# Gated linear attention: decayed q and k halves in one tile per level on VectorE, the rank-16 gate in one product, filling products in smaller pieces

## The chip, the cores and the metric

The kernel runs on one core of a Trainium2 chip. The metric is the device time of one execution in microseconds. TensorE (PE) does the matrix products, VectorE (DVE), ScalarE (ACT) and GpSimd (POOL) work on tiles of 128 partitions, SyncE (SP) starts the loads. [...]

## What is computed

Two transformer-like blocks over 512 tokens of width 1024, in fp32. The change lies in the first mixer of the second block, a gated linear attention (GLA) with 4 heads, keys of 128 and values of 256 per head:

```python
def gla_mixer(h, w_in, w_gate, b_gate, g_out, w_out):
    proj = h @ w_in                               # q, k, v, r and a rank-16 part glr
    log_a = log_sigmoid(glr @ w_gate + b_gate) / 16
    o = gla_chunked(q * DK**-0.5, k, v, log_a)
    o = rmsnorm(o, g_out) * silu(r)
    return o @ w_out

# in gla_chunked, for each chunk of 64 tokens, b = cumsum(log_a) in the chunk:
attn[i, j] = sum_c q[i, c] * k[j, c] * exp(b[i, c] - b[j, c])     # j <= i
o = (q * exp(b)) @ state + attn @ v
state = state * exp(b_last) + (k * exp(b_last - b)).T @ v
```

Before it in the same kernel stand a convolution mixer, a mixture of 16384 small experts and a gated projection; behind it an MLP, a latent attention and a second MLP.

## The kernel before

Activations lie transposed, 128 channels on the partitions and the 512 tokens along the free dimension. A product in full precision is three passes (`mm3`, L229 to L233): each operand is split into a high part in the fast fp32r format and the rest (`h`, `lo`), and high x high, low x high and high x low are added in PSUM. Weights come as blocks of 16 units of 128 x 128 through `Stream` (L75); `load_split` (L208) copies a block in two chunks to the high part on ACT (L214) and subtracts on POOL (L215) for the rest. Two blocks' splits fit in memory. PSUM has four accumulators `mm` (`ps`), two `sm` (`psm`) and two `gg`.

`gla_mix` (L1023) takes the normalized input `hs` in two halves of the tokens. `early` does projections 0 to 3 (q and k of heads 0 and 1) and beside them `low` (L1079), the rank-16 projection of 16 columns, also in three passes. Then come projection 4, the gate products of the four heads (L1095, plain fp32 on 16 rows), the log-sigmoid as Abs, Exp, Ln on ACT (L1099 to L1104), its running sum `b` within a chunk as a scan on DVE (L1107), and projections 5 and 6.

The scores with decay are built in `gla_decay` (L1149) without an exponential of a positive number: for each of six levels `s` = 32, 16, 8, 4, 2, 1 the tokens are cut into pairs of neighbouring runs of `s`; a query in the second run and a key in the first meet at the reference, the last token of the first run. `parts` (L1160) computes the distance `d` of `b` to that reference for both halves (two DVE subtractions, L1169 and L1170), takes the exponential (L1171), and multiplies q by it on DVE (`ql`, L1173) and k on POOL (`kl`, L1174), both over all 512 tokens. Four products of 128 x 128 (L1187) give a group of scores in PSUM, and a copy under a mask (L1192; the first level multiplies by its mask, L1190) takes from it what belongs to the level. The seventh step uses q and k themselves and the mask of the diagonal. The parts of the next level are computed ahead of the scores of this one. At the end come the decayed k and q for the state (L1194 to L1202) and a transpose. `gla_chain` (L1210) multiplies scores and state with v; `gate` (L1118) normalizes and multiplies with silu of r.

`weave` (L128) writes the order by hand: it steps through generators and after every n-th step calls a filling function, a v block `v_(n, half)` (48 products for four token tiles, whose sums `vp` occupy all four `mm` accumulators until the second half is done) or an r projection `r_(n)` (24 products). This order is a priority, not the order of execution: a planner fixes each engine's order at compile time, from its own estimate of when operands are ready, and may take later work first.

## Time and profile before

| | us |
|---|---|
| median of 3 runs | 3233.8 |
| lowest and highest | 3232.93, 3239.72 |
| the profiled execution | 3239.99 |
| its span, first to last instruction | 3238.2 |
| TensorE matmul busy | 3064.1 (95%) |
| mean granted clock | 0.973 |

The profile is one execution. A timeline row gives the start and the duration in us, the engine, the line of the kernel, the operation, output <- inputs, how many, and in brackets how long the engine was idle before and who released it. A group row gives busy time and mean ns of one, then the idle time before the group. Matmuls overlap, so the distance between two starts tells their cost, not their duration. The linear attention up to its output projection takes about 1978 to 2224 us.

### The profile page before, as it was taken

The numbers are of one execution on the slowest core, as the hardware profiler recorded it, in microseconds if no ns is written. First come the engines' busy times: TensorE is split into PE (matmuls) and PEld (weight loads), VectorE is DVE, ScalarE is ACT, GpSimd is POOL, SyncE is SP. The second block draws the span as 40 slices with busy tenths as digits, with TensorE's granted clock in tenths as the row PEclk, the third lists the DMA queues.
The fourth block names the chain that finished last, engine by engine and source line by source line (L and its number), as shares of the span: only waits on it lengthen the run. The fifth ranks groups of instructions, "written<-read, shape, count | busy, mean of one in ns | idle before, by whom it ended". The sixth has DMA issues, their size and how long they took to land.

```text
span 3238.2 us, 38828 instructions
## 1 busy us (share of the span) xinstructions
PE 3064.1 (95%) x15428; PEld 2552.4 (79%) x15428; DVE 1910.5 (59%) x3262; ACT 1056.2 (33%) x1632; POOL 1446.8 (45%) x777
## 2 busy tenths in 40 slices
PE   8599998889999999999999988899999999999998
PEld 7488887677888888887777777678888887888887
DVE  8974778986545555556888556765311267552123
ACT  4232223444332222322222245343322234442222
POOL 5635666222444444444444443533445431244444
PEclk9799999999999999999999998899999999999999
DMA  3122333655544544446776321111222221122321
GB/s 134 71 79 105 117 117 124 234 208 221 185 172 169 182 169 171 167 157 241 255 267 222 107 78 60 65 40 66 91 85 104 98 78 48 53 79 84 117 87 64
DMA packets 131062, 418.59 MB, mean 129 GB/s; under 512 B 7728, under 2 KB 73776, under 8 KB 97088
## 3 DMA queue, kind: packets, MB, share of 16 engines
q1 hardware_dynamic: 130880, 416.11, 36.4%
q8 instruction: 121, 1.98, 0.2%
q14 instruction: 61, 0.50, 0.0%
HBM read 364.70 MB, written 51.38 MB: 128 GB/s over the span
## 4 chain that ended last, share of the span: by engine, by line
PE 67%; DVE 13%; DMA 2%; issue 2%; ACT 1%; POOL 1%; DVEq 0%; POOLq 0%; ACTq 0%
PE mm L231 21%; PE mm L233 20%; PE mm L232 20%; DVE a L627 2%; DMA a<-act_d 2%; DVE al L630 2%; PE gg L845 2%; DVE og L827 1%; DVE o L822 1%; DVE x L641 1%; DVE l L378 1%; PE sm L1223 1%; DVE aw L926 1%; PE sm L1187 1%; DVE sq L295 0%
## 5 line engine op out<-in xcount | busy, mean ns | idle before, releaser
L215 POOL TENSOR_TENSOR wl<-raw,wh 128x1024 fp32r<-128x1024 f32 (+4 forms) x526 | 1261.5, 2421 | 1608.1 <-ACT wh L214 1596.4
L231 PE MATMUL mm<-h,wh 128*128 128x512 f32 (+1 forms) x2524 | 963.5, 382 | 27.0 <-DVE x L964 7.5
L233 PE MATMUL mm<-h,wl 128*128 128x512 f32 (+1 forms) x2524 | 956.6, 380 | 23.6 <-POOL wl L215 23.5
L232 PE MATMUL mm<-l,wh 128*128 128x512 f32 (+1 forms) x2428 | 927.7, 382 | 16.5 <-DVE l L226 12.1
L214 ACT CAST wh<-raw 128x1024 fp32r<-128x1024 f32 (+4 forms) x526 | 509.9, 996 | 1038.8 <-PE mm L232 543.6
L231 PEld LDWEIGHTS mm<-h,wh 128*128 128x128 f32 x2524 | 484.4, 192 | 114.6 <-DVE x L964 8.7
L233 PEld LDWEIGHTS mm<-h,wl 128*128 128x128 f32 x2524 | 483.6, 192 | 113.1 <-POOL wl L215 27.5
L232 PEld LDWEIGHTS mm<-l,wh 128*128 128x128 f32 x2428 | 465.5, 192 | 101.0 <-DVE l L226 12.9
L231 PE MATMUL mm<-ah,wh 128*128 128x512 f32 x1024 | 401.2, 392 | 12.8 <-DVE x L641 12.7
L233 PE MATMUL mm<-ah,wl 128*128 128x512 f32 x1024 | 400.6, 391 | 0.0
L232 PE MATMUL mm<-al,wh 128*128 128x512 f32 x1024 | 400.2, 391 | 0.0
L627 DVE TENSOR_TENSOR a<-a,g 128x512 f32<-128x512 f32 x128 | 189.0, 1498 | 261.7 <-ACT a L612 194.1
L231 PEld LDWEIGHTS mm<-ah,wh 128*128 128x128 f32 x1024 | 193.5, 189 | 56.9 <-issue 14.5
L641 DVE TENSOR_TENSOR x<-x,mm 128x512 f32<-128x512 f32 x256 | 171.0, 679 | 100.4 <-PE mm L233 100.2
L233 PEld LDWEIGHTS mm<-ah,wl 128*128 128x128 f32 x1024 | 193.1, 189 | 40.5
L232 PEld LDWEIGHTS mm<-al,wh 128*128 128x128 f32 x1024 | 193.4, 189 | 40.1
L1472 DVE TENSOR_TENSOR sg<-sg,mm 128x512 f32<-128x512 f32 (+1 forms) x48 | 30.9, 643 | 301.0 <-PE mm L233 288.0
L630 DVE TENSOR_TENSOR al<-a,ah 128x512 fp32r<-128x512 f32 x128 | 176.4, 1394 | 36.5 <-ACT ah L629 34.8
L964 DVE SCALAR_TENSOR_TENSOR x<-mm,mod,x 128x256 f32<-128x256 f32 (+1 forms) x112 | 66.5, 594 | 188.5 <-PE mm L233 188.4
L926 DVE CUSTOM_DVE_ANT_0 aw<-aw,c 128x1024 f32<-128x1024 f32 x96 | 149.5, 1557 | 11.0 <-DMA aw<-in_ada_w 11.0
L629 ACT CAST ah<-a 128x512 fp32r<-128x512 f32 x128 | 79.4, 621 | 220.7 <-PE mm L233 125.4
L231 PE MATMUL mm<-g,wh 128*128 128x512 f32 (+1 forms) x416 | 148.6, 357 | 0.0
(391 smaller groups left out, 3770.0 us busy)
## 6 DMA issues: line engine op xcount, KB each, us to landing
raw<-in_expert_u SPq DMA_DIRECT2D x64, 1024.0 KB, 4.9
raw<-in_expert_v SPq DMA_DIRECT2D x64, 1024.0 KB, 6.9
aw<-in_ada_w SPq DMA_DIRECT2D x96, 512.0 KB, 5.8
raw<-in_ffn_w_in SPq DMA_DIRECT2D x44, 1024.0 KB, 4.8
g_d<-gs SPq DMA_DIRECT2D x16, 2048.0 KB, 7.2
g<-g_d SPq DMA_DIRECT2D x32, 1024.0 KB, 6.4
act_d<-a SPq DMA_DIRECT2D x15, 1024.0 KB, 3.9
a<-act_d SPq DMA_DIRECT2D x15, 1024.0 KB, 4.8
```

The lines of the kernel that those rows point to most:

```text
L214: self.keep(nc.scalar.copy(h[:, c], raw[:, c]))
L215: nc.gpsimd.tensor_tensor(lo[:, c], raw[:, c], h[:, c].bitcast(F32), ALU.subtract)
L231: nc.tensor.matmul(out, w[0], x[0], start=start, stop=False)
L232: nc.tensor.matmul(out, w[0], x[1], start=False, stop=False)
L233: nc.tensor.matmul(out, w[1], x[0], start=False, stop=stop)
L627: nc.vector.tensor_tensor(v3(a), v3(a), g4[:, :, j, :], ALU.mult)
L629: nc.scalar.copy(h, a)
L630: nc.vector.tensor_tensor(lo, a, h.bitcast(F32), ALU.subtract)
L641: nc.vector.tensor_tensor(X[n], X[n], p, ALU.add)
L845: nc.tensor.matmul(p[:, i * P : (i + 1) * P], o1[:, t, :], og[j][:, t, :], start=(j == 0), stop=(j == 1))
L926: nc.vector.tensor_tensor_reduce(w, w, c, 1.0, 0.0, ALU.mult, ALU.add, self.mod[:, i : i + 1])
L964: self.nc.vector.scalar_tensor_tensor(x, p, self.mod[:, o + n : o + n + 1], x, ALU.mult, ALU.add)
```

## The change

Five things. `gla_decay` keeps one tile `d` per level: one DVE subtraction gives b minus the reference for both halves; the exponential is taken per half with its sign; then the first half is multiplied with k and the second with q, in place and on DVE. The scores of a level multiply the tile with itself, and the masked copy reads and writes the second halves alone. The diagonal comes first instead of last. The gate is one fp32r product on 80 rows: `w_lr` holds the 16 columns three times (at 0, 32 and 64, zeros between), so the projection gives three copies of `glr`, of which two are the high part and the third the rest, against the gate weights' high part, rest and high part. `v_` and `r_` become lists of smaller pieces (12 products each) and are handed to `weave` in another distribution, with `v_(1, 1)` behind `r_(0)` and `r_(1)`. Projection 7 is written ahead of the decay.

```diff
@@ -1027,12 +1028,15 @@
         hs = pre.hs
         masks = gl.tile([P, len(LEVELS) + 1, P], F32, tag="masks", name="masks")
         nc.sync.dma_start(masks, self.A["masks"][:, : len(LEVELS) + 1, :])
-        wg, rm = self.e("v", 8), self.e("v", 8)
-        nc.sync.dma_start(wg[:16], self.A["gla_w_gate"])
-        wl, wlh, wll = self.e("o", 4), self.e("o", 4, F32R), self.e("o", 4, F32R)
-        nc.sync.dma_start(wl[:, :P], self.A["gla_w_lr"])
-        nc.scalar.copy(wlh[:, :P], wl[:, :P])
-        nc.vector.tensor_tensor(wll[:, :P], wl[:, :P], wlh[:, :P].bitcast(F32), ALU.subtract)
+        wg, wgs, rm = self.e("v", 8), self.e("v", 8, F32R), self.e("v", 8)
+        nc.sync.dma_start(wg[:RG], self.A["gla_w_gate"])
+        nc.scalar.copy(wgs[:RG], wg[:RG])
+        lo = slice(32, 48)
+        nc.vector.tensor_tensor(wgs[lo], wg[lo], wgs[lo].bitcast(F32), ALU.subtract)
+        wl, wlh, wll = (gl.tile([P, KD, RG], dt, tag=t, name=t) for t, dt in (("lr", F32), ("lrh", F32R), ("lrl", F32R)))
+        nc.sync.dma_start(wl, self.A["gla_w_lr"])
+        nc.scalar.copy(wlh, wl)
+        nc.vector.tensor_tensor(wll, wl, wlh.bitcast(F32), ALU.subtract)
         nc.vector.memset(rm, 1.0)
         nc.vector.memset(rm.rearrange("p (c t) -> p c t", t=GCH)[:, :, 0:1], 0.0)
         sq, sv, sr = Stream(self, "gla_w_qk"), Stream(self, "gla_w_v"), Stream(self, "gla_w_r")
@@ -1049,50 +1053,56 @@
         def qk_(n):
             return lambda: evict(n, self.proj(sq, n * KD, hs))

-        vp = []
+        vp = [None] * NT

         def v_(n, half):
-            def f():
+            def f(t):
                 if half == 0:
-                    vp[:] = [self.ps() for _ in range(NT)]
-                for t, p in enumerate(vp):
-                    sl = slice(t * P, (t + 1) * P)
-                    for kk in range(half * KD // 2, (half + 1) * KD // 2):
-                        w = sv.unit(n * 32 + 4 * kk, 4)
-                        self.mm3(p, (hs[kk][0][:, sl], hs[kk][1][:, sl]), w, kk == 0, kk == KD - 1)
-                    if half:
-                        vt[t][n] = self.e("v", 8)
-                        nc.scalar.copy(vt[t][n], p)
-
-            return f
+                    vp[t] = self.ps()
+                sl = slice(t * P, (t + 1) * P)
+                for kk in range(half * KD // 2, (half + 1) * KD // 2):
+                    w = sv.unit(n * 32 + 4 * kk, 4)
+                    self.mm3(vp[t], (hs[kk][0][:, sl], hs[kk][1][:, sl]), w, kk == 0, kk == KD - 1)
+                if half:
+                    vt[t][n] = self.e("v", 8)
+                    nc.scalar.copy(vt[t][n], vp[t])
+
+            return [lambda t=t: f(t) for t in range(NT)]
+
+        rp = []

         def r_(n):
-            def f():
-                p = self.proj(sr, n * KD, hs)
-                rs[n] = self.e("r", 4)
-                nc.scalar.activation(rs[n], p, AF.Silu)
-
-            return f
+            def f(half):
+                if half == 0:
+                    rp.append(self.ps())
+                for k in range(half * KD // 2, (half + 1) * KD // 2):
+                    self.mm3(rp[-1], sr.unit(n * KD + k), hs[k], k == 0, k == KD - 1)
+                if half:
+                    rs[n] = self.e("r", 4)
+                    nc.scalar.activation(rs[n], rp[-1], AF.Silu)
+
+            return [lambda half=half: f(half) for half in range(2)]

         zp = []

         def low(k, sl):
             if k == 0:
-                zp.append(self.psm()[:16, :HS])
-            c = slice(k * 16, k * 16 + 16)
-            self.mm3(zp[-1], (wlh[:, c], wll[:, c]), (hs[k][0][:, sl], hs[k][1][:, sl]), k == 0, k == KD - 1)
+                zp.append(self.psm()[:RG, :HS])
+            self.mm3(zp[-1], (wlh[:, k, :], wll[:, k, :]), (hs[k][0][:, sl], hs[k][1][:, sl]), k == 0, k == KD - 1)

         self.early(sq, pre, evict, low)
-        glr = self.e("v", 8)
+        glr = self.e("v", 8, F32R)
+        lo = slice(64, RG)
         for z, sl in zip(zp, HALVES):
-            nc.scalar.copy(glr[:16, sl], z)
+            nc.scalar.copy(glr[:RG, sl], z)
+            nc.vector.tensor_tensor(glr[lo, sl], z[lo], glr[lo, sl].bitcast(F32), ALU.subtract)
         qk_(4)()
         for f in pre.later:
             f()
         lm = []
         for h in range(GH):
             z = self.psm()
-            nc.tensor.matmul(z, wg[:16, h * P : (h + 1) * P], glr[:16], start=True, stop=True)
+            nc.tensor.matmul(z, wgs[:RG, h * P : (h + 1) * P], glr[:RG], start=True, stop=True)
             bg = self.col("gla_b_gate", h)
             b.append(self.e(f"h{h}", 4))
             lm.append(self.e("v", 8))
@@ -1107,6 +1117,7 @@
             nc.vector.tensor_tensor_scan(a, rm, m, 0.0, ALU.mult, ALU.add)
         qk_(5)()
         qk_(6)()
+        qk_(7)()
         at, el = [None] * GH, [None] * GH

         def decay(h):
@@ -1132,12 +1143,12 @@
             yield
             yield from chain(nxt)

-        weave([decay(0)], [qk_(7), v_(0, 0)], 2)
-        weave([decay(1)], [v_(0, 1), v_(1, 0)], 3)
-        weave([decay(2), chain(0)], [v_(1, 1), r_(0), r_(1)], 2)
-        weave([decay(3), after(0, 1)], [r_(2), r_(3)], 3)
-        weave([gate(1), chain(2)], [r_(4), r_(5)], 2)
-        weave([gate(2), chain(3)], [r_(6), r_(7)], 2)
+        weave([decay(0)], v_(0, 0), 2)
+        weave([decay(1)], v_(0, 1), 2)
+        weave([decay(2), chain(0)], v_(1, 0) + r_(0))
+        weave([decay(3), after(0, 1)], r_(1) + v_(1, 1) + r_(2))
+        weave([gate(1), chain(2)], r_(3) + r_(4))
+        weave([gate(2), chain(3)], r_(5) + r_(6) + r_(7))
         late = []

         def rest():
@@ -1151,45 +1162,50 @@

         nc = self.nc
         c4 = lambda a, s: a.rearrange("p (n two s) -> p n two s", two=2, s=s)
-        v3 = lambda a: a.rearrange("p (t i) -> p t i", t=NT)
         at = at_[h] = self.e(f"h{h}", 4)
         nch = S // GCH
         b3 = bh.rearrange("p (c t) -> p c t", t=GCH)
         last = b3[:, :, GCH - 1 : GCH]

-        def parts(li):
-            if li == len(LEVELS):
-                return qh, kh
-            s = LEVELS[li]
+        def level(s):
+
+
             n = S // (2 * s)
             b4 = c4(bh, s)
-            ref = b4[:, :, 0, s - 1 : s].to_broadcast([P, n, s])
             d = self.g(name="d")
             d4 = c4(d, s)
-            nc.vector.tensor_tensor(d4[:, :, 1, :], b4[:, :, 1, :], ref, ALU.subtract)
-            nc.vector.tensor_tensor(d4[:, :, 0, :], ref, b4[:, :, 0, :], ALU.subtract)
-            nc.scalar.activation(d, d, AF.Exp, scale=1.0 / 16)
-            ql, kl = self.e("ql", 3), self.g(name="kl")
-            nc.vector.tensor_tensor(ql, qh, d, ALU.mult)
-            nc.gpsimd.tensor_tensor(kl, kh, d, ALU.mult)
-            return ql, kl
-
-        nxt = parts(0)
-        yield
-        for li in range(len(LEVELS) + 1):
-            ql, kl = nxt
-            if li < len(LEVELS):
-                nxt = parts(li + 1)
-                yield
+            ref = b4[:, :, 0, None, s - 1 : s].to_broadcast([P, n, 2, s])
+            nc.vector.tensor_tensor(d4, b4, ref, ALU.subtract)
+            for i in range(2):
+                nc.scalar.activation(d4[:, :, i, :], d4[:, :, i, :], AF.Exp, scale=(2 * i - 1) / 16)
+            for i, x in enumerate((kh, qh)):
+                nc.vector.tensor_tensor(d4[:, :, i, :], d4[:, :, i, :], c4(x, s)[:, :, i, :], ALU.mult)
+            return d
+
+        def scores(k, q):
             p = self.psm()
             for t in range(NT):
                 sl = slice(t * P, (t + 1) * P)
-                nc.tensor.matmul(p[:, sl], kl[:, sl], ql[:, sl], start=True, stop=True)
-            mk = masks[:, li, None, :].to_broadcast([P, NT, P])
-            if li == 0:
-                nc.vector.tensor_tensor(v3(at), v3(p), mk, ALU.mult)
-            else:
-                nc.vector.copy_predicated(v3(at), mk.bitcast(U32), v3(p))
+                nc.tensor.matmul(p[:, sl], k[:, sl], q[:, sl], start=True, stop=True)
+            return p
+
+        nxt = level(LEVELS[0])
+        p = scores(kh, qh)
+        eye = masks[:, len(LEVELS), None, :].to_broadcast([P, NT, P])
+        nc.vector.tensor_tensor(
+            at.rearrange("p (t i) -> p t i", t=NT), p.rearrange("p (t i) -> p t i", t=NT), eye, ALU.mult
+        )
+        yield
+        for li, s in enumerate(LEVELS):
+            d = nxt
+            if li + 1 < len(LEVELS):
+                nxt = level(LEVELS[li + 1])
+                yield
+            p = scores(d, d)
+            four = lambda a: a.rearrange("p (t n two s) -> p t n two s", t=NT, two=2, s=s)[:, :, :, 1, :]
+            mk = masks[:, li, :].rearrange("p (n two s) -> p n two s", two=2, s=s)[:, None, :, 1, :]
+            mk = mk.to_broadcast([P, NT, P // (2 * s), s])
+            nc.vector.copy_predicated(four(at), mk.bitcast(U32), four(p))
         d = self.g(name="d")
         nc.vector.tensor_tensor(
             d.rearrange("p (c t) -> p c t", t=GCH), last.to_broadcast([P, nch, GCH]), b3, ALU.subtract
@@ -1628,8 +1644,13 @@
         [w[:, o + h * P : o + (h + 1) * P] for h in range(GH) for o in (0, 512)], 1)))
     A["gla_w_v"] = _blocks(_units_moving(w[:, 1024:2048]))
     A["gla_w_r"] = _blocks(_units(w[:, 2048:3072]))
-    A["gla_w_lr"] = w[:, 3072:].reshape(KD, P, 16).transpose(1, 0, 2)
-    A["gla_w_gate"] = I["gla_w_gate_2"][0]
+    thrice = np.zeros((KD, P, RG), np.float32)
+    gate = np.zeros((RG, 512), np.float32)
+    for o in (0, 32, 64):
+        thrice[:, :, o : o + 16] = w[:, 3072:].reshape(KD, P, 16)
+        gate[o : o + 16] = I["gla_w_gate_2"][0]
+    A["gla_w_lr"] = thrice.transpose(1, 0, 2)
+    A["gla_w_gate"] = gate
     A["gla_w_out"] = _blocks(_units_parts(I["gla_w_out_2"][0]))
     A["positions"] = I["positions_2"]
     w = I["mla_w_in_2"][0]
```

## Rows read from the trace of the kernel before

**Rows 1.** Page: busy time, share of the span and instructions of the engines.

```profile
PE 3064.1 (95%) x15428; PEld 2552.4 (79%) x15428; DVE 1910.5 (59%) x3262; ACT 1056.2 (33%) x1632; POOL 1446.8 (45%) x777
```

**Rows 2.** Stretches: length, busy PE, PEld, DVE, ACT, POOL, clock, DMA share, GB/s.

```profile
2026.40:2060.60 34.20, 25.35 (x126) 20.61 (x125) 27.42 (x33) 11.61 (x18) 21.04 (x11) 0.90 0.26 92
...
2083.90:2112.30 28.40, 24.55 (x105) 18.38 (x103) 12.64 (x16) 6.98 (x11) 9.11 (x5) 0.82 0.11 38
...
2112.30:2143.40 31.10, 28.69 (x172) 24.05 (x173) 25.17 (x40) 16.32 (x23) 16.68 (x9) 1.00 0.18 65
...
2143.40:2176.00 32.60, 32.60 (x179) 25.04 (x180) 21.74 (x43) 17.28 (x24) 10.68 (x6) 0.95 0.01 4
```

**Rows 3.** Timeline of PE: neighbouring 512-column products at both clock levels.

```profile
2010.27 0.39 PE L232 MATMUL mm<-l,wh 128*128 128x512 f32 x1
...
2010.50 0.40 PE L233 MATMUL mm<-h,wl 128*128 128x512 f32 x1
...
2100.52 0.63 PE L231 MATMUL mm<-wh,h 128*128 128x512 f32 x1
...
2100.95 0.63 PE L232 MATMUL mm<-wl,h 128*128 128x512 f32 x1
```

**Rows 4.** Timeline of PE: where it waited.

```profile
2030.50 1.31 PE L1187 MATMUL sm<-ql,kl 128*128 128x128 f32 x8 [4.05 <-POOL kl L1174]
...
2090.29 0.66 PE L1207 MATMUL sm<-ident,d 128*128 128x128 f32 x4 [2.48 <-DVE h L1192]
...
2143.34 0.62 PE L335 MATMUL sm<-ident,ry 128*128 128x128 f32 x4 [2.35 <-DVE ry L327]
```

**Rows 5.** Timeline of DVE, 2026 to 2127.

```profile
2026.08 0.41 DVE L1169 TENSOR_TENSOR d<-h 128x256 f32<-128x256 f32 x1
...
2029.24 1.48 DVE L1169 TENSOR_TENSOR d<-h 128x256 f32<-128x256 f32 x1
...
2039.56 2.42 DVE L1169 TENSOR_TENSOR d<-h 128x256 f32<-128x256 f32 x1
...
2050.71 0.73 DVE L1192 COPY_PREDICATED h<-masks,sm 128x512 f32<-128x512 uint32 x1
...
2083.18 0.69 DVE L1202 TENSOR_TENSOR h<-h,h 128x512 f32<-128x512 f32 x1
...
2126.73 0.69 DVE L1194 TENSOR_TENSOR d<-h 128x512 f32<-128x512 f32 x1
```

**Rows 6.** Timeline of POOL, 2028 to 2056.

```profile
2028.68 1.77 POOL L1174 TENSOR_TENSOR kl<-h,d 128x512 f32<-128x512 f32 x1 [3.07 <-ACT d L1171]
...
2039.31 2.39 POOL L215 TENSOR_TENSOR wl<-raw,wh 128x1024 fp32r<-128x1024 f32 x1 [2.54 <-ACT wh L214]
...
2050.20 5.59 POOL L215 TENSOR_TENSOR wl<-raw,wh 128x1024 fp32r<-128x1024 f32 x2
```

**Rows 7.** Groups from 2000 to 2225: busy us, mean ns, idle before.

```profile
L1174 POOL TENSOR_TENSOR kl<-h,d 128x512 f32<-128x512 f32 x24 | 36.3, 1511 | 59.5 <-ACT d L1171 33.0 <-PE sm L1187 22.7 <-PE mm L233 3.9
...
L215 POOL TENSOR_TENSOR wl<-raw,wh 128x1024 fp32r<-128x1024 f32 x22 | 56.0, 2555 | 70.9 <-ACT wh L214 63.7 <-PE sm L1187 7.2
...
L289 ACT ACTIVATE sq<-o 128x256 f32<-128x256 f32 x16 | 5.5, 418 | 0.0
```

**Rows 8.** Timeline of PE: the fourth gate product.

```profile
2011.28 1.12 PE L1095 MATMUL sm<-v,v 16*128 16x512 f32 x2
```

**Rows 9.** Timeline of ACT: the fourth Abs, a weight copy.

```profile
2013.20 0.67 ACT L1099 ACTIVATE h<-sm,cols 128x512 f32<-128x512 f32 x1
...
2018.71 1.03 ACT L214 CAST wh<-raw 128x1024 fp32r<-128x1024 f32 x1
```

**Rows 10.** Groups of PE from 2007 to 2030.

```profile
L231 PE MATMUL mm<-h,wh 128*128 128x512 f32 x24 | 9.5, 395 | 0.0
```

**Rows 11.** The chain that ended last: start, us, what.

```profile
2132.34 1.80 PE sm L1187 x16
```

More of the change, by code (lines that the diff above doesn't have):

```diff
@@ L47 @@
 GCH = 64
+RG = 80
 LEVELS = (32, 16, 8, 4, 2, 1)
```

## Prediction

> **What bounds the kernel now.** TensorE is busy 95% of the span [rows 1], so a gain can only be a stretch in which it waits, works at the lower clock, or does work that falls away. I first looked for such stretches in and around the linear attention (about 1978 to 2224 us) with the table of stretches, which gives busy time and granted clock side by side [rows 2]. From 2026.4 to 2060.6 PE is busy 25.35 of 34.20 us at clock 0.90; from 2083.9 to 2112.3 it is 24.55 of 28.40 at 0.82; from 2112.3 to 2143.4 it is 28.69 of 31.10 at full clock; from 2143.4 to 2176 it is always busy, at 0.95. [...] Two neighbouring 512-column products start 0.23 us apart at the upper level and 0.43 us apart at the lower [rows 3], so a microsecond of work at the lower level throws away half. Each lower stretch follows waits of PE, whose releasers the timeline names: 4.05 us for a `kl` of POOL, 2.48 us for a masked copy of DVE, 2.35 us for the last step of a reciprocal root on DVE [rows 4].
>
> So these stretches are set by the decay, not by PE. Its rhythm is in DVE's timeline [rows 5]: the first subtraction of a level starts at 2026.08, the next level's at 2029.24, a round of 3.2 us. Inside it DVE waits 0.69 us for the exponential, and the next subtraction, which takes 0.41 us alone, takes 1.48 us. POOL's timeline shows why [rows 6]: `kl` runs from 2028.68 to 2030.45, and the subtraction ends just after. DVE is held while POOL works. The same shows at 2039.56 (2.42 us for a 0.41 us subtraction) under the weight split that POOL began at 2039.31. The masked copy at 2050.71, whose second tensor lies in PSUM, takes its usual 0.73 us though POOL is in a split from 2050.20 on. POOL spends 36.3 us on `kl` and 56.0 us on splits here [rows 7].
>
> **Part by part.**
>
> *POOL's product goes to DVE, in halves.* Per level the old round has two subtractions of 256, one exponential of 512, one DVE product of 512 and the POOL product (24 in all, 1.51 us mean [rows 7]). The new one has a subtraction of 512 (0.69 us, as the broadcast subtraction at 2126.73 [rows 5]), two exponentials of 256 (0.42 us each, as the squares of that size [rows 7]) and two products of 256 (0.41 us each, as a subtraction of that size; back to back they start 0.34 us apart). If the second exponential runs under the first product, a round is 0.69 + 0.42 + 0.41 + 0.34 = 1.9 us with the handovers; if both products wait for both exponentials, which write interleaved halves of one tile, it is 2.2 us. The masked copy reads half as many columns: 0.73 less the 0.28 us between a 512 and a 256 operation is 0.45 us. It fits into the wait for the exponential or adds itself, so a round lies between 1.9 and 2.7 us; I take 2.2, since a copy mostly finds that wait. Six rounds are 13.2 us; with the diagonal and the three products at the end (four of 0.69 us) a head takes DVE 16 us. The splits stay, four to six in the first two heads; each can hold DVE for nothing or for all of its 2.5 us. I take half: 6 us. Two heads are 38 us. Now they take from 2026.08 to 2083.87 [rows 5], 58 us.
>
> The smallest level reads every second column of PSUM, which no row here shows; I price it like a dense copy of 256. [...]
>
> *The gate in one product.* The old gate products are fp32 and show as two records each, 1.12 us a pair [rows 8]; the new ones take a 512-column pass, 0.23 us [rows 3]. Four of them save 3.5 us of PE. The two extra subtractions on 16 partitions (256 columns, 0.41 us) stand behind the eviction of `zp` and in front of the gate; projection 4 (24 products of 0.23 us, 5.5 us of PE) hides them; without that cover they cost 0.8 us. The fourth Abs runs at 2013.20 because PE came to the fourth gate product late [rows 9]; with short products it can run about 4 us earlier. I let the decay begin at 2022 instead of 2026.
>
> *The wider rank-16 weights.* `w_lr` grows from 128 to 640 columns: its DVE subtraction to about 0.83 us (0.69 for 512 columns [rows 5] and 128 more), its ACT copy alike, and `w_gate` adds a copy on ACT and a subtraction of 512 columns on DVE. Together at most 1.5 us on each of them near 1978, where the second half of the normalization also passes. It costs nothing if it falls in DVE's holes, 2.5 us if the chain stands behind all of it and behind a load that I allow 1 us more, which no row shows; I take 1. The products themselves have 80 columns instead of 16 in the stationary operand and the same 256 moving; I cost that at nothing.
>
> *`qk_(7)` ahead of the decay.* Worth nothing: the planner already runs it there. Between 2007 and 2030 PE does 24 products of each of the three kinds [rows 10], which is projections 5, 6 and 7.
>
> *Smaller filling pieces.* No PE work changes. A v block was 48 products, 11 us at 0.23, between two levels; now a score product waits behind 12, 2.7 us. But the first two heads have two v blocks instead of three. Their PE work is 2 x 11 + 2 x 7 score groups of 0.9 us (16 records in 1.80 us [rows 11]) + 1.3 for transposes, about 36 us. PE is through its projections at 2026.4 - 3.5 = 2023 and could end them at 2059; DVE ends them at 2022 + 38 = 2060. The two meet.
>
> *Sum.* Up to the end of head 1: 2083.9 - 2060 = 24 us earlier, with one v block (11 us) not yet done and three score groups and a transpose (3.3 us) done in addition: 16 us. That would close every gap there, and PE and DVE would have to interleave perfectly; I take 10. With a head at 26 us (2.7 us rounds, every split held in full) it is 2. Behind head 1: idle 3.85 and 2.41 us and half of 10.2 + 3.3 us at the lower clock, 13 us in all [rows 2]; the wait for the reciprocal root is untouched and the clock may fall again, so I take 7, with bounds of 0 and 13. Less 1 (0 to 2.5) for the set-up: 16 us, bounds 0 and 29. The profiled execution took 3239.99 us, so 3224.0; it was 6.2 us above the median of the runs, on which the forecast stands: 3217.8.
>
> **The rivals.**
>
> *The filling is held up by PSUM* (0.29). `r_(0)` now stands between `v_(1, 0)` and `v_(1, 1)`. All four `mm` accumulators then hold open v sums until `v_(1, 1)`, so `r_(0)` and `r_(1)` can't start, `gate(0)` waits for them, and the second weight slot is taken by a block that can't be used. The next v block is split only after `v_(1, 0)`: a copy of 1.03 us [rows 9] and a POOL split of 2.56 us [rows 7] stand open. Against it: the planner moves work that is ready, as it did with `qk_(7)`, and `chain(0)` can fill. Price: the 7 us behind head 1 and 3.6 us: 3228.4, within 3224 to 3232.
>
> *DVE stays as slow as it is* (0.13), which is slower than before. All three DVE operations of the new round have two tensors in SBUF and are open to being held by a split, and the first two heads have one v block less under them. If their 58 us stay, head 1 ends at 2080 with 11 us of v left over and 3.3 us done: 3.7 us lost; with the set-up's 2.5 and one more fall of the clock (3.4 us at half) about 8 us are lost: 3242. It decides from about 54 us for two heads. Against it: in the old round each `kl` alone holds DVE for 1.1 us, and these 24 holds go. [...]
>
> *Everything closes* (0.11): 16 + 13 and no set-up cost: 3205, within 3204 to 3212.
>
> **How the numbers follow.** Forecast, 3212 to 3224: 0.47. Within 0.2% (6.5 us, about what a measurement of this kernel can tell from no change) lies what ends between 3227.3 and 3240.3. Of the PSUM rival 0.10 is faster than that and 0.19 within it. Faster 0.47 + 0.11 + 0.10 = 0.68, same 0.19, slower 0.13. The range 3206 to 3236 leaves out the slower rival and the edge of the best one.
>
> **What would show it.** Right: rounds of about 2.2 us between the new 512-wide subtractions; no POOL product in the stretch; four gate products of one record; PE idle below 8 us between 2026 and the first output product, and at most one fall of the clock. The PSUM rival shows as Silu evictions of `r_(0)` only after the last v eviction; the slower one as subtractions and products of 1.5 us and more under the splits. Wrong at the root: if the part before 1960 or behind the output projection moves, since nothing of the change lies there.

## The result and the profile after

The changed kernel takes 3206.73 us (median of 5 runs, 3202.11 to 3215.19) where the kernel before takes 3233.8 (5 runs, 3232.71 to 3244.94): the two medians divide to 0.9916, and the ratio on record with its interval is 0.9928, 0.9909 to 0.9947. The forecast was 3217.8, the range 3206 to 3236. The direction came out as forecast and the mechanism in the main; the gain is larger than its 16 us, and the median lies only 0.7 us inside the range.

The profiled execution after took 3206.3 us (span 3204.5), the one before 3239.99 (span 3238.2). I split this difference at two marks that lie outside every edit: the first product of the spread (`sm<-ident,ry`, which brings the reciprocal root to all partitions) of the normalization's first half ahead of the attention, and the first of the spread of its second half ahead of the MLP. What lies between is called **the stage** from here on. Before, it runs from 1955.15 to 2275.34, which is 320.19 us. PE's timeline of the kernel after:

```profile
1943.58 1.00 PE L336 MATMUL sm<-ident,ry 128*128 128x128 f32 x4 [4.61 <-DVE ry L328]
...
2243.02 0.40 PE L336 MATMUL sm<-ident,ry 128*128 128x128 f32 x2
```

That is 299.44 us, so 20.75 us of the 33.7 us between the spans were gained in the stage. Of the rest, 11.6 us lie ahead of it and 1.4 us behind it. Ahead of it the instructions of every engine stand in the same order in both kernels, and later runs put the start anywhere from 1939 to 1960 us whatever was edited (the same kernel once more: 1946.16). So I take the 11.6 us for a difference between executions and compare stages; that is argued, not shown, and what makes the executions differ there stays open.

Where PE stood in the stage, from its records (gaps between them; half of the time in which it worked at the lower clock; the remainder as work at full clock): before 27.0 + 13.3 + 279.9 us, after 17.5 + 9.8 + 272.1. Half, because the granted clock, a share of its upper level, reads 0.50 in the falls (after: 2022.3 to 2025.6 and 2233.9 to 2240.6; before: 2096 to 2102) and 1.00 between the two of after (2025.8 to 2233.7). Each of the three fell: waits by 9.5, clock by 3.5, work by 7.8.

The stretches of the kernel after (length; busy PE, PEld, DVE, ACT, POOL; granted clock; DMA share; GB/s), which answer to [rows 2]: the first two heads of the decay, the third, the fourth, and from there into the output projection.

```profile
2015.70:2049.20 33.50, 30.17 (x171) 26.05 (x170) 29.99 (x57) 17.75 (x40) 9.88 (x4) 0.95 0.22 81
2049.20:2086.00 36.80, 34.25 (x206) 27.82 (x205) 21.38 (x38) 13.49 (x28) 9.87 (x4) 1.00 0.13 45
2086.00:2114.10 28.10, 28.10 (x150) 22.62 (x148) 19.98 (x47) 16.07 (x26) 5.22 (x2) 1.00 0.08 28
2114.10:2196.90 82.80, 80.87 (x433) 65.24 (x433) 38.53 (x78) 26.30 (x43) 21.88 (x9) 1.00 0.17 61
```

PE is idle 3.3, 2.6, 0 and 1.9 us in them, and only the first has a lower clock (0.95 of 33.5 us is 3.4 us at the lower level). The stretch at 0.82 and the one at 0.95 of [rows 2] are gone.

DVE's timeline after, which answers to [rows 5]:

```profile
2015.71 1.26 DVE L1178 TENSOR_TENSOR d<-h 128x512 f32<-128x512 f32 x2
2016.89 1.42 DVE L1182 TENSOR_TENSOR d<-d,h 128x256 f32<-128x256 f32 x4
2018.24 1.28 DVE L1178 TENSOR_TENSOR d<-h 128x512 f32<-128x512 f32 x2
...
2021.56 0.45 DVE L1208 COPY_PREDICATED h<-masks,sm 128x256 f32<-128x256 uint32 x1
2021.91 2.31 DVE L1178 TENSOR_TENSOR d<-h 128x512 f32<-128x512 f32 x1
2024.14 0.44 DVE L1208 COPY_PREDICATED h<-masks,sm 128x256 f32<-128x256 uint32 x1
2024.47 2.54 DVE L1178 TENSOR_TENSOR d<-h 128x512 f32<-128x512 f32 x1
...
2032.46 0.73 DVE L1208 COPY_PREDICATED h<-masks,sm 128x256 f32<-128x256 uint32 x1 [0.37 <-PE sm L1189]
...
2041.54 2.30 DVE L1178 TENSOR_TENSOR d<-h 128x512 f32<-128x512 f32 x1
...
2048.51 0.68 DVE L1218 TENSOR_TENSOR h<-h,h 128x512 f32<-128x512 f32 x1
```

Two levels go through DVE together: two subtractions, then their four products, and the next pair of subtractions starts 2.53 us after the first (2015.71, 2018.24), without a wait for an exponential. Two heads last from 2015.71 to 2049.19: 33.5 us, against 57.8 before. What still holds DVE are the weight splits: POOL's timeline has

```profile
2007.49 5.50 POOL L216 TENSOR_TENSOR wl<-raw,wh 128x1024 fp32r<-128x1024 f32 x2 [11.39 <-ACT wh L215]
2021.30 5.16 POOL L216 TENSOR_TENSOR wl<-raw,wh 128x1024 fp32r<-128x1024 f32 x2 [8.31 <-ACT wh L215]
```

Under the second line the two subtractions take 2.31 and 2.54 us instead of 0.68, while the masked copy between them, which reads PSUM, takes its 0.44.

### The profile page after: what moved, and what is told of

It reads as the page before. It is cut to its first block, busy times and chain, and to the rows that moved or that the text cites. A ratio compares the mean times of both kernels' runs of the same rounds, so it can differ in the third digit from the quotient of the medians.

```text
span 3204.5 us, 38766 instructions
## 1 busy us (share of the span) xinstructions
PE 3047.0 (95%) x15424; PEld 2549.7 (80%) x15424; DVE 1869.2 (58%) x3265; ACT 1051.2 (33%) x1651; POOL 1420.9 (44%) x753
## 4 chain that ended last, share of the span: by engine, by line
PE 73%; DVE 8%; ACT 1%; issue 1%; DMA 0%; POOL 0%; DVEq 0%; POOLq 0%; ACTq 0%
PE mm L232 23%; PE mm L234 23%; PE mm L233 23%; PE gg L846 2%; DVE og L828 1%; DVE o L823 1%; PE sm L1189 1%; DVE l L379 1%; DVE sq L296 0%; DVE m L370 0%; PE sm L1239 0%; DMA a<-act_d 0%; PE sm L306 0%; PE gg L1266 0%; PE gg L1260 0%
## 5 line engine op out<-in xcount | busy, mean ns | idle before, releaser
L628 DVE TENSOR_TENSOR a<-a,g 128x512 f32<-128x512 f32 x128 | 155.4, 1236 | 247.8 <-ACT a L613 194.5
L631 DVE TENSOR_TENSOR al<-a,ah 128x512 fp32r<-128x512 f32 x128 | 165.4, 1308 | 36.4 <-ACT ah L630 34.7
L927 DVE CUSTOM_DVE_ANT_0 aw<-aw,c 128x1024 f32<-128x1024 f32 x96 | 171.4, 1786 | 10.1 <-DMA aw<-in_ada_w 10.1
L232 PE MATMUL mm<-g,wh 128*128 128x512 f32 (+1 forms) x416 | 148.6, 357 | 0.0
L233 PE MATMUL mm<-g,wh 128*128 128x512 f32 (+1 forms) x416 | 148.2, 356 | 0.0
```

Source lines behind the costliest of these rows:

```text
L232: nc.tensor.matmul(out, w[0], x[0], start=start, stop=False)
L233: nc.tensor.matmul(out, w[0], x[1], start=False, stop=False)
L628: nc.vector.tensor_tensor(v3(a), v3(a), g4[:, :, j, :], ALU.mult)
L631: nc.vector.tensor_tensor(lo, a, h.bitcast(F32), ALU.subtract)
L927: nc.vector.tensor_tensor_reduce(w, w, c, 1.0, 0.0, ALU.mult, ALU.add, self.mod[:, i : i + 1])
```

## The experiments

All of them are compared by the stage (one trace each) and by the ratio to the kernel before with its interval. The two agree: the difference of stages, divided by 3240 us, lies within the interval of the ratio, or at its edge (a_only, k_half_on_pool), for every kernel below. The fourth column is the time from the first subtraction of the decay to the end of the last product of its second head; the fifth is what DVE waited for score products ahead of its 24 masked copies, from the groups of DVE.

The stage has parts that no edit of the decay or of the filling touches, and they aren't equally long in all traces: from its start to the spread of the second half 27.7 to 30.2 us, its last part, from the first half's spread ahead of the MLP, 18.0 to 19.5 us, by where the clock falls. Between the two, ahead of the decay, the clock is at its lower level for 13.7 us in kl_on_dve and 10.2 in c_only, elsewhere for at most 3.4. The third column, **decay to MLP**, runs from the first subtraction of the decay to the first half's spread ahead of the MLP and leaves these parts out. There is one trace of each kernel (two of after), so no difference of 2 or 3 us in either column is shown to be the edit's.

| kernel | ratio [95%] | stage, us | decay to MLP, us | two heads, us | DVE waits for scores, us |
|---|---|---|---|---|---|
| before | 1 | 320.19 | 231.19 | 57.8 | 9.4 |
| after | 0.9928 [0.9909, 0.9947] | 299.44 | 207.85 | 33.5 | 18.2 |
| after_again | 0.9932 [0.9909, 0.9955] | 299.49 | 207.88 | | |
| a_only: new decay | 0.9970 [0.9955, 0.9985] | 315.44 | 223.71 | 49.1 | 40.4 |
| c_only: new filling | 1.0033 [1.0017, 1.0048] | 330.86 | 239.51 | 53.6 | 15.9 |
| a_c: decay and filling | 0.9942 [0.9924, 0.9959] | 299.76 | 209.96 | 34.1 | 17.8 |
| a_b: decay and gate | 0.9975 [0.9957, 0.9994] | 311.64 | 221.43 | 46.9 | 39.1 |
| blocks_new_place | 0.9964 [0.9946, 0.9981] | 309.37 | 219.15 | 43.6 | 29.6 |
| pieces_old_place | 0.9915 [0.9885, 0.9945] | 295.33 | 205.20 | 42.1 | 22.0 |
| r_behind_v | 0.9922 [0.9899, 0.9946] | 299.75 | 209.57 | | |
| kl_on_dve | 0.9989 [0.9971, 1.0008] | 320.21 | 228.05 | 55.2 | 5.2 |
| kl_on_dve_c | 1.0020 [1.0004, 1.0036] | 327.08 | 237.32 | 60.7 | 18.4 |
| k_half_on_pool | 0.9922 [0.9896, 0.9948] | 303.44 | 212.41 | | |
| v_split_on_dve | 0.9912 [0.9883, 0.9942] | 291.81 | 205.79 | 33.7 | 14.5 |

**Which part earns it.** First the kernel after once more, for what an execution does by itself; then before with the new `gla_decay` alone (a_only) and with the new filling alone (c_only: pieces, their places, `qk_(7)`); then after with the old gate (a_c) and with the old filling (a_b). The gate alone wasn't run.

> The changed kernel once more, unchanged. If the 11.8 us by which the profiled execution of after was ahead at the start of the stage (1937.14 against 1948.92 at the same product) are a property of the program, this execution starts the stage within 3 us of 1943.6 again; if they are chance of the execution, it may start 5 to 15 us off. The stage itself: 298 to 302.

Measured: 299.49 us of stage, 0.05 from the first trace, from a start 2.6 us later. By the bound set for it, 3 us, that start speaks for a property of the program. But all kernels here run the same work ahead of the stage, and with the old gate they start anywhere from 1939.4 to 1960.1 us, with the new one from 1939.1 to 1950.6, so two executions don't settle it.

```
-  old body of gla_decay          (a_only: this alone)
+  new body of gla_decay
```

> The kernel before with the new gla_decay alone (one tile per level, all on DVE, diagonal first, half-width masked copies); gate, projection 7 and the filling as before. The stage meant here and below runs from the spread of the normalization's first half ahead of the attention (1955.15 in the trace before, 1943.58 after) to that of the second half ahead of the MLP (2275.34 and 2243.02): 320.2 us before, 299.4 after. Theory, the decay's rhythm of DVE and POOL is what was lost: stage 305 to 310, so two thirds or more of the 20.8 us come back without the rest. Rival, the filling in large blocks is what starved PE: stage 313 to 319, since scores still wait behind 48 products.

Measured: 315.44 us, in the second theory's range. From the decay to the MLP it is 7.5 us quicker than before, which would put the stage at the edge between the two. The decay became quicker and was then stopped by the filling. DVE's and PE's timelines of a_only:

```profile
2052.42 0.44 DVE L1197 COPY_PREDICATED h<-masks,sm 128x256 f32<-128x256 uint32 x1 [6.21 <-PE sm L1178]
...
2073.60 0.44 DVE L1197 COPY_PREDICATED h<-masks,sm 128x256 f32<-128x256 uint32 x1 [6.22 <-PE sm L1178]
```

```profile
2051.33 1.83 PE L1178 MATMUL sm<-d 128*128 128x128 f32 x15
```

A score group stands behind a v block of 48 products, which PE runs from 2039.71 to 2051.33, and DVE waits 6.2 us for it; all such waits together are 40.4 us, against 18.2 in after.

```
-  weave([decay(0)], [qk_(7), v_(0, 0)], 2)      (c_only: filling alone)
+  qk_(7)()
+  weave([decay(0)], v_(0, 0), 2)
...
```

> The kernel before with the smaller filling pieces, their new distribution and projection 7 written earlier; decay and gate as before. Theory: the stage stays within 4 us of 320 (316 to 322), because the level round of 3.2 us with POOL's product stays and the first two heads have one v block less to cover it. Rival, large blocks starved PE: stage 305 to 311.

Measured: 330.86 us, outside both ranges and slower than before by 10.7 us, of which 8.3 lie from the decay to the MLP. Over its first two heads PE is busy 39.13 of 53.70 us at clock 0.87; before, over the two heads, 46.90 of 57.80 at 0.94. In the stretches of c_only and then of before:

```profile
2027.80:2081.50 53.70, 39.13 (x199) 32.52 (x197) 41.94 (x58) 17.11 (x28) 29.71 (x16) 0.87 0.17 59
```

```profile
2026.10:2083.90 57.80, 46.90 (x236) 38.69 (x235) 46.75 (x58) 19.88 (x31) 35.25 (x18) 0.94 0.20 73
```

PE has less filling there, two v blocks instead of three, and waits for the old rhythm, in which `kl` stands behind two splits (PE and POOL of c_only). That the third block is what is missing is argued: pieces in the old places weren't run with the old decay.

```profile
2047.39 2.08 PE L1193 MATMUL sm<-ql,kl 128*128 128x128 f32 x8 [6.15 <-POOL kl L1180]
```

```profile
2041.10 4.83 POOL L215 TENSOR_TENSOR wl<-raw,wh 128x1024 fp32r<-128x1024 f32 x2 [2.53 <-ACT wh L214]
2045.90 3.12 POOL L1180 TENSOR_TENSOR kl<-h,d 128x512 f32<-128x512 f32 x2
```

> The new decay and the new filling, the old gate (four fp32 products on 16 rows, 64 KB of rank-16 weights). Theory: the gate is worth what PE saves on its four products, 3.5 us, and the set-up costs 1: stage 301 to 303.5. Rival, the gate is what starts the decay earlier and DVE's chain then ends everything earlier: stage 306 to 310.

> The new decay and the new gate, the old filling blocks. Theory: with the decay fast the size of the pieces matters little, since PE does the same work and is behind DVE: stage 300 to 304. Rival, a score group behind 48 products (11 us) instead of 12 (2.7 us) stops DVE's chain: stage 306 to 312, with waits of DVE for L1187-like score products of several us.

Measured: a_c 299.76, just under its first range: behind decay and filling the gate is worth 0.3 us of stage. a_b 311.64, the rival's range: without the new filling 12.2 us are lost. So the decay alone gives 4.8 us of stage, the filling alone costs 10.7, and both together give 20.4; from the decay to the MLP it is 7.5, 8.3 and 21.2. What the large blocks cost shows on PE mostly as clock: from the decay to the MLP a_b has 10.1 us of waits, 10.1 of clock loss and 201.2 of work, after has 7.8, 1.7 and 198.3.

**Pieces or places.** after with the old whole blocks in the new places, and with the small pieces in the old places (how often `weave` hands one out changes with them):

```
+  whole = lambda fs: [lambda: [f() for f in fs]]         (blocks_new_place)
-  weave([decay(1)], v_(0, 1), 2)
+  weave([decay(1)], whole(v_(0, 1)), 2)
...
-  weave([decay(1)], v_(0, 1), 2)                         (pieces_old_place)
-  weave([decay(2), chain(0)], v_(1, 0) + r_(0))
+  weave([decay(1)], v_(0, 1) + v_(1, 0))
+  weave([decay(2), chain(0)], v_(1, 1) + r_(0) + r_(1))
...
```

> The changed kernel with every v half handed out as one block of 48 products again and every r as one of 24, in the new distribution. So far the new decay alone gives a stage of 315.4 us, the new filling alone 330.9, both together 299.8. If it is the size of the pieces that lets the faster decay through (a score group waits behind 2.7 instead of 11 us): stage 306 to 312. If it is the distribution, one v block less under the first two heads: stage 299 to 303.

> The changed kernel with the small pieces in the old distribution: v_(1, 0) under head 1, v_(1, 1) with r_(0) and r_(1) under head 2. Size theory: stage 298 to 302, as after. Distribution theory: 307 to 312, as the new decay and the new gate with the old blocks (311.6).

Measured: whole blocks cost 9.9 us in the new places (309.37) and 16.3 in the old (311.64 against 295.33). The places alone gain 2.3 us with whole blocks and lose 4.1 with pieces (2.6 from the decay to the MLP). 295.33 lies under both ranges, and the new places aren't shown to be a gain. So the size of the pieces is what the filling's part rests on; the 39.1 us that DVE waits for scores in a_b go to 29.6 with the new places alone and to 22.0 with the pieces alone.

**The PSUM rival.** after with `v_(1, 1)` ahead of `r_(0)`:

```
-  weave([decay(2), chain(0)], v_(1, 0) + r_(0))
-  weave([decay(3), after(0, 1)], r_(1) + v_(1, 1) + r_(2))
+  weave([decay(2), chain(0)], v_(1, 0) + v_(1, 1) + r_(0))
+  weave([decay(3), after(0, 1)], r_(1) + r_(2))
```

> The changed kernel with v_(1, 1) handed out ahead of r_(0) instead of behind r_(0) and r_(1). In after r_(0) waits until the first sum of v_(1, 1) leaves PSUM, and PE is idle 2.6 us between 2080.7 and 2084.9 around the split of that block. If the held accumulators and the occupied weight slot cause this wait, it goes: stage 296.5 to 298.5. If the planner already took what was ready and the wait is DVE's (held by the split itself), the stage stays at 299 to 300.

Measured: 299.75 us, no gain. PE's wait of 2.6 us is gone, as the first theory has it, but PE waits 2.1 us from 2112.0 on instead, after which the clock is at its lower level for 6.8 us. So the other order gains nothing in sum; what the hold costs by itself isn't shown. It exists in after, as ACT's timeline shows:

```profile
2090.71 0.59 ACT L1068 COPY v<-mm 128x512 f32<-128x512 f32 x1 [0.19 <-PE mm L234]
2097.11 0.60 ACT L1082 ACTIVATE r<-mm 128x512 f32<-128x512 f32 x1 [1.98 <-PE mm L234]
...
2119.34 0.59 ACT L1068 COPY v<-mm 128x512 f32<-128x512 f32 x1 [6.00 <-PE mm L234]
```

The Silu of `r_(0)` comes after the first eviction of the last v block, and its first product starts at 2091.43, just behind that eviction, so it did wait for an accumulator; but with the v evictions one by one it doesn't wait for the last, and PE is never idle from 2086.0 to 2114.1 (the third stretch above).

**Engine or narrower work.** Is POOL's product to blame, or the number of instructions? before with `kl` on VectorE, nothing else; the same with the new filling; and after with half of the products on GpSimd:

```
-  nc.gpsimd.tensor_tensor(kl, kh, d, ALU.mult)           (kl_on_dve, kl_on_dve_c)
+  nc.vector.tensor_tensor(kl, kh, d, ALU.mult)
...
+  eng = nc.vector if i else nc.gpsimd                    (k_half_on_pool)
-  nc.vector.tensor_tensor(d4[:, :, i, :], d4[:, :, i, :], c4(x, s)[:, :, i, :], ALU.mult)
+  eng.tensor_tensor(d4[:, :, i, :], d4[:, :, i, :], c4(x, s)[:, :, i, :], ALU.mult)
```

> The kernel before with one word changed: the product kl runs on VectorE instead of GpSimd, full width. It takes away the holds by POOL's products (24 of 1.1 us on DVE) and adds 24 products of 0.69 us to DVE. Theory, the hold and POOL's slow product are what the old round lost: a round is 0.7 + 0.63 + 0.69 + 0.6 = 2.7 instead of 3.2 us, stage 310 to 316. Rival, what counts is the smaller width of the operations (halves instead of full products and copies): no gain, stage 318 to 324.

> The kernel before with kl on VectorE and with the new filling, old gate: it parts the new decay into the engine of the k product and the rest (halves, one subtraction, half-width masked copies, diagonal first). The engine alone left the stage at 320.2, the new filling alone made it 330.9. If the engine is what matters once the filling is in small pieces: stage 300 to 307. If the narrower work on DVE is: 314 to 326, since DVE then has 24 x 0.69 us more instead of less.

> The changed kernel with the product of the k half (256 columns, strided) on GpSimd again, the q half on VectorE. Theory: POOL takes about 0.75 us for it and holds DVE's next subtraction or product; a round grows by 0.4 to 0.9 us and DVE's chain is late again: stage 303 to 308. Rival, the halves were the gain and the engine is of no matter: stage 298 to 301.

Measured: kl_on_dve has the shorter round that was expected, 2.66 us instead of 3.2, and yet 320.21 us of stage, the rival's range. DVE's timeline of it:

```profile
2017.29 0.42 DVE L1169 TENSOR_TENSOR d<-h 128x256 f32<-128x256 f32 x1
...
2019.95 0.42 DVE L1169 TENSOR_TENSOR d<-h 128x256 f32<-128x256 f32 x1
...
2027.57 2.89 DVE L1174 TENSOR_TENSOR kl<-h,d 128x512 f32<-128x512 f32 x1
```

The splits, which held the subtractions before, now hold `kl` too, and two heads take 55.2 us. But the stage judges this kernel too hard. From the second half's spread to the decay, where it doesn't differ from before, PE takes 3.7 us longer at a lower clock (stretches of kl_on_dve and of before):

```profile
1967.56:2013.51 45.95, 45.06 (x216) 34.82 (x217) 22.73 (x35) 26.49 (x42) 15.29 (x6) 0.85 0.13 47
```

```profile
1983.81:2026.08 42.27, 41.37 (x228) 33.07 (x228) 22.55 (x35) 26.29 (x42) 15.44 (x6) 1.00 0.15 51
```

From the decay to the MLP the move alone gives 3.1 us, between what the two theories had, and the whole new decay gives 7.5. With the new filling the stage is 327.08, just above the range of the narrower work, and the move gives 3.8 us of stage and 2.2 from the decay to the MLP. So the move from POOL to VectorE alone gives 0 to 4 us, and most of the gain comes with the rest of the new decay: half as many elements per level (one tile of 512 in place of `ql` and `kl` of 512 each, a copy of 256 in place of 512), one subtraction, the diagonal first. These weren't run apart. The other way, POOL takes half of the products again and loses 4.0 us of stage (303.44, as expected of the holds), so 16.75 of the 20.75 us are there with the k half still on POOL; the whole runs cannot tell that kernel from after. DVE and POOL of k_half_on_pool:

```profile
2025.34 1.81 DVE L1183 TENSOR_TENSOR d<-d,h 128x256 f32<-128x256 f32 x2
```

```profile
2024.75 2.98 POOL L1183 TENSOR_TENSOR d<-d,h 128x256 f32<-128x256 f32 x3 [3.92 <-ACT d L1180]
```

**The splits.** after, with the low part of the v blocks' weights subtracted on VectorE:

```
-  sq, sv, sr = Stream(self, "gla_w_qk"), Stream(self, "gla_w_v"), Stream(self, "gla_w_r")
+  sq, sv, sr = Stream(self, "gla_w_qk"), Stream(self, "gla_w_v", eng=nc.vector), Stream(self, "gla_w_r")
...
-  nc.gpsimd.tensor_tensor(lo[:, c], raw[:, c], h[:, c].bitcast(F32), ALU.subtract)
+  (eng or nc.gpsimd).tensor_tensor(lo[:, c], raw[:, c], h[:, c].bitcast(F32), ALU.subtract)
```

> The changed kernel with the weight split of the v blocks (eight chunks of 1024 columns) on VectorE, about 1.2 us each, instead of 2.4 to 2.8 us each on GpSimd. In after two chunks at 2007.49 and 2010.15 hold two DVE operations of the gate for 2.83 and 2.88 us, and two at 2021.30 and 2023.62 hold two subtractions for 2.30 and 2.54. If these holds delay the first levels and leave PE waiting 3.3 us around 2017 to 2021.5: stage 295 to 298. If DVE has no room for the 10 us of splits: 300 to 305.

Measured: 291.81 us of stage, 7.6 under after and below both ranges. Of these, 1.4 lie in the stage's last part, where the clock falls for 6.8 us in after and for 3.4 here; 4.3 come from the earlier start of the decay. DVE's timeline of it:

```profile
2014.40 1.27 DVE L1117 TENSOR_TENSOR v<-v,h 128x512 f32<-128x512 f32 x2
...
2017.84 1.27 DVE L1179 TENSOR_TENSOR d<-h 128x512 f32<-128x512 f32 x2
...
2020.36 2.35 DVE L217 TENSOR_TENSOR wl<-raw,wh 128x1024 fp32r<-128x1024 f32 x2
2022.63 1.28 DVE L1179 TENSOR_TENSOR d<-h 128x512 f32<-128x512 f32 x2
```

A split takes 1.2 us here, half of POOL's 2.5, and the subtractions behind it have their own length again. By the whole run its interval overlaps with that of after, so a version that beats the changed kernel isn't proved. It and the pieces in the old places weren't run together.

## Why the prediction was right, and where it was too small

The decay's rhythm was what PE waited for, as forecast, but making it quicker paid in full only together with the small pieces, and most of the terms fell inside their bounds. Two things were luck. Head 1 ends 23.1 us earlier in the stage, where the forecast had 24, but two errors cancel there: the decay starts 1.2 us later in the stage instead of 4 earlier, and its first two heads take 24.3 us less instead of 20. And the median lies 6.3 us lower than the stage's gain would put it (3233.8 less 20.75 is 3213.0), by what lies outside the stage, which is taken for scatter here.

**Round and decay.** Forecast: a round of 1.9 to 2.7 us, taken 2.2; two heads in 38. Measured: 1.27 us a level (2.53 for a pair) where no split disturbs, two heads in 33.5. What failed is the lower bound of the round: it was the length of one level's own sequence, subtraction, exponential, product. The trace of after runs two levels in each other's gaps, so a level costs DVE only its own instructions (half of 1.26 and half of 1.42 us, which overlap a little); its masked copy comes later, among others. The half-width copy came out as forecast, 0.44 against 0.45. The splits were sized well: three subtractions held for 2.31, 2.54 and 2.30 us in two heads, 1.6 to 1.9 each over their own length, so about 5 us against 6.

**Earlier start.** Forecast: 4 us earlier through the short gate products. It failed. From the first Abs to the first subtraction of the decay are 19.5 us before and 19.1 after. The four products did shrink to one record each, and all Abs were done 3.7 us after the first one instead of 6.7. PE's timeline of after, which answers to [rows 8]:

```profile
1995.87 0.63 PE L1105 MATMUL sm<-v,v 80*128 80x512 f32 x2
1998.20 0.40 PE L1105 MATMUL sm<-v,v 80*128 80x512 f32 x1
1998.89 0.40 PE L1105 MATMUL sm<-v,v 80*128 80x512 f32 x1
```

But DVE then meets the two splits from 2007.49 on, and two subtractions of the gate's log-sigmoid are held (in the kernel before one is, 2.82 us):

```profile
2007.91 5.62 DVE L1116 TENSOR_TENSOR v<-v,h 128x512 f32<-128x512 f32 x2
```

The same operation takes 1.27 us for two in v_split_on_dve, where this chain is 14.8 us long. I had counted splits in the first two heads only. PE's saving is there all the same, 3.1 us (3.5 forecast), but a_c against after shows that 0.3 of it is left in the stage: the set-up is 1.4 us longer in after than in a_c, and PE waits longer for the first scores (3.3 us in after, 2.05 in a_c).

**Set-up.** Forecast: 1 us. Measured from the stage's start to the second half's spread: 28.66 before, 29.53 after, 0.9. Kernels with the old gate take 27.66 to 30.02 there, so this is within what traces differ by.

**Up to the end of head 1.** Forecast: 10 us taken (2 to 16). From the second half's spread to the end of head 1 PE's waits fell from 11.8 to 4.2 us, its clock loss rose from 2.5 to 3.3 and its work fell from 85.8 to 68.6. Of that work, 58 products of v blocks (13.6 us at their mean of 0.235) only moved behind head 1, where the forecast had 11 us, and 9 records of scores (1.0 us) moved ahead, where it had 3.3. So 4.6 us of work fell away, 3.1 of them at the gate, and this part gained 11.4 us.

**Behind head 1.** Forecast: 7 us (0 to 13). The 10.2 and 3.3 us at the lower clock in its sum follow from [rows 2], 28.4 us at 0.82 and 32.6 us at 0.95, with the 0.50 measured above. Waits fell from 10.3 to 7.3 and clock loss from 6.8 to 3.1, which is 6.7 us, near the forecast. But another 3.5 us of work fell away with the moved products taken out, so this part gained 10.2 us. This is the term that was sized too small. Work was priced at nothing but the gate; in the whole stage 4.7 us more of it went, in steps between products too short to be seen as waits (those of the chain's products alone went from 36.9 to 34.7 us). As the forecast allowed, the clock falls again later, at 2233.8 ahead of the MLP for 6.8 us, which the kernel before doesn't have there; the traces of after_again and a_c have it too, those of pieces_old_place and r_behind_v don't.

**The filling.** The forecast has it that the two "meet", about 36 us of PE work against 38 of DVE, and prices the pieces with the decay in one sum. The runs show that this sum can't be taken apart into edits: −4.8 and +10.7 make −20.4 (−7.5 and +8.3 make −21.2 from the decay to the MLP).

**The rivals.** "DVE stays as slow as it is" was the right account of another kernel: c_only keeps the old decay under the new filling and is 10.7 us slower in the stage (8.3 from the decay to the MLP), where the rival had 8, 2.5 of them for a set-up that c_only doesn't have. It had the loss begin at about 54 us for two heads, and c_only's take 53.6. Its sign, subtractions of over 1.5 us under splits, shows in after as well, but only three times in two heads. The PSUM rival's mechanism is seen in after, its price of 10.6 us isn't: PE's waits and clock loss behind head 1 fell by 6.7, and the other order gains nothing. "Everything closes" had 3205 with no wait left, within 3204 to 3212. The median lies in that band and not in the forecast's of 3212 to 3224, but 17.5 us of waits and 9.8 us of clock loss are still in the stage; the stage's own gain would put the kernel at 3213.0, in the forecast's band.

**What would show it.** No POOL product in the stretch: from 1990 to 2196 POOL has a single group.

```profile
L216 POOL TENSOR_TENSOR wl<-raw,wh 128x1024 fp32r<-128x1024 f32 x23 | 57.5, 2519 | 150.9 <-ACT wh L215 150.9
```

PE's waits between the decay's start and 2197, behind the first output product, are 7.8 us (below 8, from the four stretches), with one fall of the clock. The round of about 2.2 us didn't show, since two levels share it. The part before 1960 did move in the profiled pair, which I had called wrong at the root; the scatter of the starts shows that one pair of executions can't carry that test.

**The smallest levels.** I had priced their masked copies like dense ones. Measured: 0.41 to 0.45 us for levels 32 to 4, 0.71 to 0.74 for levels 2 and 1 (2032.46 above), eight copies in all, so 8 x 0.28 = 2.3 us of DVE. In PSUM the slow copies read runs of two elements or of one, but their mask and their output lie in SBUF with runs as short, so which operand makes them slow isn't shown; VectorE's products in SBUF with the same runs stay at 0.39 to 0.44 us.

## What to carry to other kernels

An engine made quicker pays only if what it alternates with comes in pieces of about its new step: the quicker decay alone gave 4.8 us of stage and waited 40 us behind 48-product blocks, and with 12-product pieces it gave 20.4. Bound a round of a pipelined loop from below by the instructions that it puts on its busiest engine, not by one round's own chain. And judge a change on marks around its stage, since the work ahead of it ended up to 21 us apart from one trace to the next, and set the marks so close that a fall of the clock in work that the edit doesn't touch stays outside: in kl_on_dve such a fall hid 3 us.

## What was not expected of the hardware

- A masked copy of 256 columns out of PSUM costs 0.71 to 0.74 us with runs of two or one elements, as much as 512 dense columns [rows 5], and 0.41 to 0.45 with runs of four and more.
- A VectorE operation with both inputs in SBUF took up to 2.89 us under a GpSimd split (kl_on_dve; in after 2.85 at 2077.94, under the split from 2077.88; alone 0.68), a masked copy out of PSUM under such a split wasn't held (0.44 us at 2024.14 in after). The split itself took 1.2 us on VectorE (v_split_on_dve) and 2.5 on GpSimd (after), so moving it shortened both.
- The clock fell to its lower level for 10.2 us in kl_on_dve at 1994.07, in the middle of 45 us of projections and 25 us after PE's last wait; the same work in the kernel before, after a wait of the same 0.89 us, ran at the upper level throughout (1.00 against 0.85 over the two stretches).
- Half of the products on GpSimd made the stage 4.0 us longer (k_half_on_pool): three of them take it 2.98 us, and two VectorE products beside them 1.81 instead of 0.75.
